# An encoder layer on one core: the order of all queues from a list scheduler inside the kernel

## The chip, the core and the metric

The kernel runs on one core of a Trainium2 chip. A core has TensorE (PE; its weight loads are shown as PEld), VectorE (DVE), ScalarE (ACT), GpSimd (POOL) and a queue on SyncE (SP) that issues nearly all transfers. Each works through its own instructions in order; semaphores tie them together. The metric is the device time of one execution in microseconds (us).

## The reference

One layer: windowed attention with a sink, and a SwiGLU feed-forward network, each between two RMS norms, with shift, scale and gate from a conditioning vector. S = 2048 tokens, D = 1024, 16 query heads and 4 key heads of 64, window of 128 tokens to both sides, hidden size 2816, all float32.

```
mod = silu(c) @ ada_w + ada_b                      # 6 x 1024: sh1, sc1, g1, sh2, sc2, g2
h   = rmsnorm(x, mix_norm_pre) * (1 + sc1) + sh1
q, k, v = split(h @ w_qkv)
logits = q k^T / 8 + bias(relative position)       # 128 queries x 384 keys, masked at +-128
p   = softmax([logits, sink])                      # the sink takes part and is dropped
x   = x + g1 * rmsnorm((p v) @ w_o, mix_norm_post)
h   = rmsnorm(x, ffn_norm_pre) * (1 + sc2) + sh2
x   = x + g2 * rmsnorm((silu(h @ w_a) * (h @ w_b)) @ w_out, ffn_norm_post)
```

## The kernel before

Activations lie transposed, features on the partitions, 512 tokens (a chunk) along the free side; there are four chunks. A float32 matmul is made from three rounded ones: each operand is split into a high part (`act.copy`) and a low part (a subtraction on VectorE or GpSimd), by `split`, lines L155 and L156, and `three`, lines L150 to L152, multiplies high by high, high by low and low by high into one PSUM bank.

The stages, in order of the program:
- The norm of chunk 0 (`nsta`, `nr`), the conditioning rows (`ada_reduce`, L263) and a first wave of q, k, v tiles (`psq`). `evac` writes q, k and v to DRAM (`q_d`, `k_d`, `v_d`), and chunks 1 to 3 follow.
- Attention: 64 units of 128 queries x 4 heads. `Unit.scores` multiplies q by k into one of two banks of the pool `psS` (`s`, L433), VectorE adds the bias and takes the maximum (L438: `pr`, `nm`), ScalarE takes the exponent (L440), GpSimd divides (L446). `Unit.values` transposes `pr` on TensorE into one of three banks (`t`, L456), splits it into `phi` and `plo` (L155, L156) and multiplies by v (`o`, L461, L462); `low` and `of` (L465, L469) put it together and write `o_d`. Between the units a budget puts in "fillers" by threes of matmuls: the q, k, v tiles of chunks 2 and 3 in the first half, the output projection (`py`, from `ol`, the loaded `o_d`, and `wo`) of chunks 0 to 2 in the second.
- The output projection of chunk 3, norms, residuals and the second normalized input `h2_d`. For chunks 2 and 3 this is done late (`late_residuals`: `ly`, `lx`, `lacc`, `nhil`, `nstl`; `ly` is multiplied by GpSimd at L508 and added to by VectorE at L509), beside the feed-forward network.
- The feed-forward network in two halves of 1024 tokens, by blocks of a 2 x 2 scheme with seven products in place of eight (`Block`, `Operands`, `Hidden`, `Outs`). Weights come in as `wiri`, sums of them as `s`, split into `wa` and `ws`; VectorE and ScalarE take the seven products out of PSUM (`take`: `p_i`, `u_i`, `b_i` for the hidden layer, `z` at L943 for the output). The hidden values go through DRAM (`g_d`).
- `finish` (L990, L991) scales each output tile and adds the residual `x1_d`.

The order of the instructions on each queue is made by the tile framework's own scheduler from the program order (the context is opened with `schedule_with_timeline_sim=True`). It is helped by hand with `tc.issue_after(...)` (an operation is held until another has been issued), `tc.high_priority(offset=...)` (it counts as that much earlier) and `tc.keep_in_program_order(...)`. Buffers are tiles of pools; a tile waits until its slot is free, pools are opened and closed in the nesting of the stages, and later pools take over the space of closed ones.

```
            for h in range(GRP):
                ps = psS.tile([P, CH], F32, tag="s", name=f"s{u}_{h}")
                ...
    psF = open_pool(ctx, "psF", 2, space=PSUM)
    psS = open_pool(att, "psS", 2, space=PSUM)
    psT = open_pool(att, "psT", 3, space=PSUM)
    psV = open_pool(att, "psV", 1, space=PSUM)
```

```
    def residual(c, k, y, xr, r, acc, alloc, eng=dve):
        sp.dma_start(xr, a["xT"][c, :, k, :])
        pool.tensor_tensor(y, y, r, ALU.mult)
        eng.tensor_tensor(y, y, xr, ALU.add)
        sp.dma_start(x1_d[c][:, k, :], y)
        ...
```

Of the kernel before, what the change touches and what calls it, by code (L numbers as in the profile page):

```python
# [11 lines left out]
F32 = mybir.dt.float32  # L12
F32R = mybir.dt.float32r
AF = mybir.ActivationFunctionType
ALU = mybir.AluOpType
# [45 lines left out]
OPERANDS = ("b11", "t2", "b21", "t3", "t1", "t4", "b22")  # L61


def f(ap):
    return ap.bitcast(F32)
# [8 lines left out]
def encoder_layer(ctx, tc, a):  # L74
# [41 lines left out]
    dve.memset(epsc, EPS)  # L116
    make_identity(nc, ident)

# [35 lines left out]
    def split(hi, lo, src, eng):  # L154
        act.copy(hi, src)  # L155
        return eng.tensor_tensor(lo, src, f(hi), ALU.subtract).ins  # L156

# [7 lines left out]
    class Chunk:  # L165
# [34 lines left out]
        def h(self, k):  # L200
            xt, c = self.xt[k], self.c
            scaled = dve.tensor_tensor(xt, xt, self.r, ALU.mult).ins
            act.activation(xt, xt, AF.Identity, bias=mod[:, k:k + 1], scale=coef[:, 0, k:k + 1])
            hi = hs.tile([P, CH], F32R, tag="hi", name=f"hi{c}_{k}")
            lo = hs.tile([P, CH], F32R, tag="lo", name=f"lo{c}_{k}")
            self.hh[k] = (hi, lo)
            return scaled, split(hi, lo, xt, dve)

    def evac(c, n, ps, psp, ptag):

        t = ev.tile([P, 2, CH], F32R, tag="e", name=f"e{c}_{n}")
        if n < KT:

            hi, lo = (t[:, i].rearrange("p (b t) -> p b t", t=P)[:, :, ::-1] for i in range(2))
            src = ps.rearrange("p (b t) -> p b t", t=P)
            act.activation(hi, src, AF.Copy, scale=DH ** -0.5)
            ins = dve.scalar_tensor_tensor(lo, src, DH ** -0.5, f(hi), ALU.mult, ALU.subtract).ins
            for j in range(2):
                h = 2 * n + j
                dst = q_d[c][h // GRP].rearrange("(i d) h t -> d i h t", i=2)[:, :, h % GRP, :]  # L220
                sp.dma_start(dst, f(t[j * DH:(j + 1) * DH]))
        elif n < KT + 2:
            ins = split(t[:, 0], t[:, 1], ps, dve)
            for j in range(2):
                for d in range(2):
                    sp.dma_start(k_d[c][2 * (n - KT) + j][d * DH:(d + 1) * DH], f(t[j * DH:(j + 1) * DH]))
        else:
            vt = nrm.tile([P, CH], F32, tag="nsq", name=f"vt{c}_{n}", bufs=2)
            act.copy(vt, ps)
            pv = psp.tile([P, CH], F32, tag=ptag, name=f"pvt{c}_{n}")  # L230
            for j in range(JB):
                pe.transpose(pv[:, j * P:(j + 1) * P], vt[:, j * P:(j + 1) * P], ident)
            t = t.rearrange("p a b -> p (a b)").rearrange("p (g j i d) -> p g j i d", g=2, j=JB, i=2)
            s = pv.rearrange("p (j g d) -> p g j d", j=JB, g=2)
            for g in range(2):
                act.copy(t[:, g, :, 0, :], s[:, g])
                ins = dve.tensor_tensor(t[:, g, :, 1, :], s[:, g], f(t[:, g, :, 0, :]), ALU.subtract).ins
                sp.dma_start(v_d[c][2 * (n - KT - 2) + g], f(t[:, g].rearrange("p j i d -> p j (i d)")))
        return ins


    with ExitStack() as pa:
# [11 lines left out]
        sp.dma_start(cb_d, cb)  # L254
        tc.keep_in_program_order(act.preload_act_table_set("natural_log_exp_and_others"))

# [25 lines left out]
        for k in range(KT):  # L282
            with tc.issue_after(steps[max(k - 2, 0)][0]) if k >= 1 else ExitStack():
                ada_reduce(*ada_load(8 + k, raws))
                ada_reduce(*ada_load(k, raws))
            dve.scalar_tensor_tensor(coef[:, 0, k:k + 1], mod[:, 8 + k:9 + k], 1.0, gains[:, 0, k:k + 1],
                                     ALU.add, ALU.mult)
            w_piece(k, 0)
            with tc.issue_after(steps[k - 2][1]) if k >= 2 else ExitStack():
                steps.append(ch0.h(k))  # L290
            for n in NORD[:WAVE]:
                three(pss[n], wres[k, n], ch0.hh[k], k == 0, k == KT - 1)
# [9 lines left out]
        def v_tile(ch, i):  # L302
# [12 lines left out]
            for m in range(2):  # L315
                t = vt[c][m][:, :, 2 * i:2 * i + 2]
                for g in range(2):
                    act.copy(t[:, g, :, 0, :], s[:, m, g])
                    ins = dve.tensor_tensor(t[:, g, :, 1, :], s[:, m, g], f(t[:, g, :, 0, :]), ALU.subtract).ins
                    if i:  # L320
                        sp.dma_start(v_d[c][2 * m + g], f(vt[c][m][:, g].rearrange("p j i d -> p j (i d)")))
# [18 lines left out]
        for i, n in enumerate(NORD[WAVE:] + NORD[:WAVE]):  # L340
            ins = qkv_tile(ch1, n)
            if i >= 2:
                with tc.issue_after(ins):
                    for w in waiting[i - 2:i - 1]:
                        ada_reduce(*w)
            if i < ADA_A:
# [64 lines left out]
    class Unit:  # L411
# [10 lines left out]
        def scores(self):  # L422
# [7 lines left out]
            for h in range(GRP):  # L430
                ps = psS.tile([P, CH], F32, tag="s", name=f"s{u}_{h}")
                for i in range(2):
                    m = pe.matmul(ps[:, :n], q[:, h, jb * P:(jb + 1) * P], kk[:, i, (jb + j0) * P:(jb + j1) * P],  # L433
                                  start=i == 0, stop=i == 1)
                    if h == i == 0:
                        self.first = m.ins
                hh = g * GRP + h
# [4 lines left out]
                if h == 0:  # L442
                    self.red = red.ins
            dve.reciprocal(rs, rs)  # L444
# [87 lines left out]
    class OProj:  # L532
# [5 lines left out]
        def fill(self, prev=None, hold=None):  # L538
# [11 lines left out]
            for n in range(KT):  # L550
# [10 lines left out]
                for k in range(KT):  # L561
                    t = o[k // 2]
                    with ExitStack() as st:
                        while hold is not None and n >= KT - HOLD and hold() is None:
                            yield None
                        if hold is not None and n >= KT - HOLD and k == 0:
                            st.enter_context(tc.issue_after(hold()))
                        three(ps, (w[:, 0, k], w[:, 1, k]), (t[:, 0, k % 2], t[:, 1, k % 2]), k == 0, k == KT - 1)
# [84 lines left out]
    for i, un in enumerate(units):  # L653
# [17 lines left out]
        if i in ADA_UNITS:  # L671
            for w in waiting:
                with tc.issue_after(un.red):
                    ada_reduce(*w)
            waiting = [ada_load(late.pop(0), ws)] if late else []
# [187 lines left out]
    def late_ada():  # L863

        for i in range(2):
# [3 lines left out]
            for t in range(5 * KT, 6 * KT):  # L869
# [10 lines left out]
                    h2_d[int(n[2]) - 1][:, 2 * k + (n[1] == "2"), :])  # L880
    with tc.high_priority(offset=1):
        half.load("b11", "t2")
# [69 lines left out]
    ops = part_ops(0, 0)  # L952
    with tc.high_priority(offset=100):
        ops.load(*OPERANDS[:2])
    with tc.high_priority(offset=400):
        block = Outs(ops, 0, 0, 0)
    for i in range(5, 7):
# [52 lines left out]

    tc.keep_in_program_order(act.preload_act_table_set("natural_log_exp_and_others"))
    NP = len(PARTS[0])
    with tc.high_priority(offset=400):
        ops.load(*OPERANDS[2:])
    end = iter(())
# [118 lines left out]
```

## Time and profile before

| | |
|---|---|
| median of 3 runs | 2156.73 us (2156.06 to 2157.14) |
| the profiled execution | 2157.47 us, span of its instructions 2155.7 us |
| TensorE busy | 95% of the span |
| VectorE, ScalarE, GpSimd busy | 76%, 50%, 34% |
| mean granted TensorE clock | 0.981 |
| moved by DMA | 396 MB, 184 GB/s |

The profile is one execution. A group of instructions is shown by its line, engine, operation and tiles (out<-in), with count, busy time, the mean duration of one in ns, the idle time of the engine ahead of them and what ended it. L150 is line 150 of the kernel. Where a table has stages, a row gives the stage in us from the start of the span, its length, the busy time of PE, PEld, DVE, ACT and POOL with the number of instructions, the granted clock, the DMA engines' busy share and GB/s.

### The profile page before, as it was taken

The numbers are of one execution on the slowest core, as the hardware profiler recorded it, in microseconds if no ns is written. First come the engines' busy times: TensorE is split into PE (matmuls) and PEld (weight loads), VectorE is DVE, ScalarE is ACT, GpSimd is POOL, SyncE is SP. The second block draws the span as 40 slices with busy tenths as digits, with TensorE's granted clock in tenths as the row PEclk, the third lists the DMA queues.
The fourth block names the chain that finished last, engine by engine and source line by source line (L and its number), as shares of the span: only waits on it lengthen the run. The fifth ranks groups of instructions, "written<-read, shape, count | busy, mean of one in ns | idle before, by whom it ended". The sixth has DMA issues, their size and how long they took to land. (4 is left out here: it accounts for less than half of the span.)

```text
span 2155.7 us, 29001 instructions
## 1 busy us (share of the span) xinstructions
PE 2037.4 (95%) x9366; PEld 1669.6 (77%) x9366; DVE 1648.5 (76%) x2933; ACT 1076.0 (50%) x2125; POOL 735.7 (34%) x687
## 2 busy tenths in 40 slices
PE   6898999999989989989999989999999999998997
PEld 4786877878777768868887867888888788877886
DVE  7656667665676669887878798777664888999987
ACT  4646666577777746343434352333332744465422
POOL 3404343367778712444354412222221000220040
PEclk9998999999999989999999999999999999999998
DMA  8887665576667695534454764323230644438442
GB/s 280 262 268 242 186 187 173 168 274 243 220 197 247 193 346 205 175 129 158 169 171 162 252 235 147 117 103 118 103 108 36 233 149 150 135 134 283 161 132 103
DMA packets 200516, 396.35 MB, mean 184 GB/s; under 512 B 20091, under 2 KB 62124, under 8 KB 195244
## 3 DMA queue, kind: packets, MB, share of 16 engines
q1 hardware_dynamic: 199788, 393.97, 54.5%
q8 instruction: 74, 1.21, 0.2%
q14 instruction: 78, 0.64, 0.1%
q10 hardware_dynamic: 576, 0.52, 0.1%
HBM read 270.65 MB, written 123.76 MB: 183 GB/s over the span
## 5 line engine op out<-in xcount | busy, mean ns | idle before, releaser
L438 DVE CUSTOM_DVE_ANT_0 pr<-s,bias,nsink 128x384 f32<-128x384 f32 (+1 forms) x256 | 149.3, 596 | 89.7 <-PE s L433 71.0
L150 PE MATMUL pc_i<-ht,ws_i 128*128 128x512 f32 x528 | 206.2, 391 | 4.9 <-DVE b_i L800 2.3
L151 PE MATMUL pc_i<-ht,ws_i 128*128 128x512 f32 x528 | 205.5, 389 | 0.0
L152 PE MATMUL pc_i<-ht,ws_i 128*128 128x512 f32 x528 | 205.3, 389 | 0.0
L440 ACT ACTIVATE pr<-pr,nm 128x385 f32<-128x385 f32 (+1 forms) x256 | 153.8, 603 | 70.7 <-DVE nm L438 65.3
L816 POOL TENSOR_TENSOR p_i<-p_i,u_i 128x512 f32<-128x512 f32 x44 | 73.5, 1671 | 307.8 <-DVE u_i L803 121.5
L446 POOL TENSOR_SCALAR pr<-pr,rs 128x384 f32<-128x384 f32 (+1 forms) x256 | 146.9, 595 | 85.3 <-DVE rs L444 85.2
L947 POOL TENSOR_TENSOR z<-z,z 128x512 f32<-128x512 f32 x32 | 53.2, 1677 | 353.0 <-DVE z L943 335.7
L433 PE MATMUL s<-k,q 128*128 128x384 f32 (+1 forms) x512 | 137.0, 361 | 21.0 <-DVE nm L438 13.7
L150 PE MATMUL pc_i<-hb,wa_i 128*128 128x512 f32 x352 | 138.1, 392 | 3.8 <-DVE u_i L790 2.6
L152 PE MATMUL pc_i<-hb,wa_i 128*128 128x512 f32 x352 | 137.5, 391 | 0.0
L151 PE MATMUL pc_i<-hb,wa_i 128*128 128x512 f32 x352 | 137.5, 391 | 0.0
L156 DVE TENSOR_TENSOR plo<-t,phi 128x512 fp32r<-128x512 f32 x184 | 121.7, 685 | 17.1 <-ACT phi L155 15.5
L155 ACT CAST ws_i<-s_i 128x512 fp32r<-128x512 f32 x132 | 81.6, 619 | 100.5 <-PE pc_i L152 91.7
L155 ACT CAST wa_i<-wiri 128x512 fp32r<-128x512 f32 x132 | 81.7, 620 | 93.8 <-PE pc_i L152 88.8
L433 PEld LDWEIGHTS s<-k,q 128*128 128x128 f32 x512 | 87.5, 195 | 45.5 <-DVE nm L438 28.1
L150 PEld LDWEIGHTS pc_i<-ht,ws_i 128*128 128x128 f32 x528 | 99.1, 188 | 28.4 <-DVE b_i L800 2.3
L456 PE MATMUL t<-ident,pr 128*128 128x128 f32 x736 | 113.7, 275 | 3.4 <-POOL pr L446 2.7
L150 PE MATMUL py<-ol,wo 128*128 128x512 f32 x256 | 103.4, 408 | 12.8 <-ACT ol L155 8.3
L152 PEld LDWEIGHTS pc_i<-ht,ws_i 128*128 128x128 f32 x528 | 99.1, 188 | 20.7
L151 PEld LDWEIGHTS pc_i<-ht,ws_i 128*128 128x128 f32 x528 | 99.1, 188 | 20.3
L156 DVE TENSOR_TENSOR wa_i<-wiri,wa_i 128x512 fp32r<-128x512 f32 x132 | 109.1, 826 | 5.1 <-ACT wa_i L155 4.9
(320 smaller groups left out, 6129.8 us busy)
## 6 DMA issues: line engine op xcount, KB each, us to landing
wiri<-w_in SPq DMA_DIRECT2D x88, 512.0 KB, 5.0
ada<-ada_w SPq DMA_DIRECT2D x40, 512.0 KB, 5.0
wiro<-w_out SPq DMA_DIRECT2D x48, 384.0 KB, 3.8
q_d<-e SPq DMA_DIRECT2D x64, 256.0 KB, 4.0
q<-q_d SPq DMA_DIRECT2D x16, 1024.0 KB, 5.4
wo<-wo_d SPq DMA_DIRECT2D x16, 1024.0 KB, 5.9
g_d_b<-p_i SPq DMA_DIRECT2D x44, 256.0 KB, 4.8
g_d_t<-p_i SPq DMA_DIRECT2D x40, 256.0 KB, 2.0
```

What stands on the lines that cost most here:

```text
L150: pe.matmul(ps, w[0], h[0], start=first, stop=False)
L151: pe.matmul(ps, w[0], h[1], start=False, stop=False)
L152: pe.matmul(ps, w[1], h[0], start=False, stop=last)
L155: act.copy(hi, src)
L156: return eng.tensor_tensor(lo, src, f(hi), ALU.subtract).ins
L433: m = pe.matmul(ps[:, :n], q[:, h, jb * P:(jb + 1) * P], kk[:, i, (jb + j0) * P:(jb + j1) * P], start=i == 0, stop=i == 1)
L438: red = dve.tensor_tensor_reduce(pr[:, h, :n], ps[:, :n], bias[g][:, h, j0 * P:j1 * P], -1.0, nsink[:, hh:hh + 1], ALU.add, ALU.min, nm[:, ...
L440: act.activation(pr[:, h, :n + 1], pr[:, h, :n + 1], AF.Exp, bias=nm[:, h:h + 1], scale=-1.0, accum_out=rs[:, h:h + 1])
L446: pool.tensor_scalar(pr[:, h, :n], pr[:, h, :n], rs[:, h:h + 1], 1.0, ALU.mult, ALU.mult)
L456: pe.transpose(pt[:, h * P:(h + 1) * P], pr[:, h, jj * P:(jj + 1) * P], ident)
L816: pool.tensor_tensor(sa, sa, b, ALU.mult)
L947: (pool if (i, x) in ((2, 2), (4, 4), (5, 5), (6, 6)) else dve).tensor_tensor(sums[hf, n2, x], sums[hf, n2, x], sums[hf, n2, y], ALU.add)
```

## The change

The computation is written as before, but against a recorder. `Recorder` stands in for the framework: every call on an engine becomes an `Op` with the regions that it reads and writes, its predecessors, and a cost from fixed constants. `place` gives every pool's tag an address by the nesting of the pools, so that closed pools' space is used again. `schedule` orders all operations on five queues in up to six rounds: `forward` is a list scheduler that always starts the operation that can start first, the more urgent one where several are ready; it gives tiles their slots, lets a VectorE operation with two SBUF inputs and a GpSimd operation not run at once (`port`), counts ScalarE's table loads, eight DMAs under way and a DMA rate; `backward` then gives each operation the latest start that the schedule allows, which is its priority in the next round. The round with the shortest planned time is kept. `emit` issues the operations in that order, with the framework's own ordering switched off (`manual_schedule`); the framework still places the semaphores. The hand-written `issue_after`, `high_priority` and `keep_in_program_order` are gone.

```
+    def cost(self, op, outs, ins):
+        ...
+        if eng == "sp":
+            op.bytes = int(np.prod(outs[0].shape)) * 4
+            op.occ, op.lat = 430, 0
+        elif eng == "pe":
+            ...
+                op.occ = n * 0.4167 + 13.5
+                op.lat = op.occ + 200
+        elif eng == "act":
+            op.occ = n / 1.2 + (51 if psum else 93)
+            op.lat = op.occ + 105
+            ...
+        elif eng == "dve":
+            fast = fn in ("tensor_copy", "tensor_scalar") and not psum
+            op.occ = n / (1.92 if fast else 0.96) + 66
+            op.lat = op.occ + 88
+            ...
+            op.port = n > P and (fast or len(sbuf) > 1)
+        else:
+            op.port = fn != "custom"
+            if fn == "tensor_tensor":
+                op.occ = n * 2.21 + 95
+                op.lat = op.occ + 45
+    ...
+    def forward(self):
+            ...
+                o = item[2]
+                if o.port:
+                    begin = max(begin, port["pool" if e == "dve" else "dve"])
+                if best is None or begin < best[0]:
+                    best = begin, e, o, src, item
+            ...
+            if e == "sp":
+                lanes.sort()
+                begin = max(begin, lanes[0])
+                first = max(begin + 1200, dma)
+                dma = first + max(o.bytes / 345.0, 100.0)
+                end = dma + 900
+                lanes[0] = end
+                lanes.sort()
+            else:
+                end = begin + o.lat
+                if o.port:
+                    port[e] = begin + o.occ
+            clock[e] = begin + o.occ
+    ...
+    def schedule(self, rounds):
+        self.place()
+        for o in self.ops:
+            o.prio = float(o.i)
+        best = None
+        for i in range(rounds):
+            order, total = self.forward()
+            if best is None or total < best[1]:
+                best = order, total, {b: b.slot for b in self.bufs.values()}
+            ...
+            if i + 1 < rounds:
+                late = self.backward(order, total)
+                for o in order:
+                    o.prio = late[o]
+        self.slots = best[2]
+        return best[0]
+    def emit(self, nc, tc, order, outside):
+        ...
+        with tc.manual_schedule():
+            for o in order:
+                if o.table == "log" and table != "log":
+                    nc.scalar.preload_act_table_set("natural_log_exp_and_others")
+                table = o.table or table
+                args, kw = [turn(x) for x in o.args], {k: turn(x) for k, x in o.kw.items()}
+                ...
+                    getattr(engs[o.eng], o.fn)(*args, **kw)
 
         for k in range(KT):
-            with tc.issue_after(steps[max(k - 2, 0)][0]) if k >= 1 else ExitStack():
-                ada_reduce(*ada_load(8 + k, raws))
-                ada_reduce(*ada_load(k, raws))
+            ada_reduce(*ada_load(8 + k, raws))
+            ada_reduce(*ada_load(k, raws))
...
-    with tc.high_priority(offset=100):
-        half.load(*[n for n in OPERANDS if n not in ("b11", "t2")])
+    half.load(*[n for n in OPERANDS if n not in ("b11", "t2")])
...
-    with tile.TileContext(nc, schedule_with_timeline_sim=True) as tc:
-        encoder_layer(tc, aps)
+    rec = Recorder(bacc())
+    ...
+    order = rec.schedule(ROUNDS)
+    ...
+    with tile.TileContext(nc) as tc:
+        rec.emit(nc, tc, order, given)
```

More of the change, by code (lines that the diff above doesn't have):

```diff
@@ L61, with __init__ @@
 OPERANDS = ("b11", "t2", "b21", "t3", "t1", "t4", "b22")
+ROUNDS = 6
+SBUF_LEFT = 1152
+SBUF_RIGHT = 229344
+BANKS = 8
+BANK = 2048
+ENGINES = ("pe", "act", "dve", "pool", "sp")
+class Op:
+    __slots__ = ("i", "eng", "fn", "args", "kw", "reads", "writes", "occ", "lat", "port", "table", "tiles", "pred", "succ",
+                 "start", "end", "prio", "npred", "ready", "ins", "bytes")
+class Buf:
+    def __init__(self, rec, name, shape, dtype, pool, tag):
+        self.name, self.shape, self.dtype, self.pool, self.tag = name, list(shape), dtype, pool, tag
+        self.row = int(np.prod(shape[1:]))
+        self.unit = 1 if self.row <= P else DH
+        self.log, self.ops, self.slot, self.real = [], set(), None, None
@@ L880, in encoder_layer @@
                     h2_d[int(n[2]) - 1][:, 2 * k + (n[1] == "2"), :])
-    with tc.high_priority(offset=1):
-        half.load("b11", "t2")
+    half.load("b11", "t2")
     lasto.close()
@@ L952, in encoder_layer @@
     ops = part_ops(0, 0)
[L953 to L956, printed above, removed]
+    ops.load(*OPERANDS[:2])
+    block = Outs(ops, 0, 0, 0)
     for i in range(5, 7):
```

437 lines of the change are left out of this document (413 added, 24 removed).

## The prediction

> **What bounds the kernel now.** I read the page first (who is busy), then the table by stage (where TensorE is idle and at what clock), then the waits of TensorE, then the timeline around the long ones.
>
> ```profile
> span 2155.7 us, 29001 instructions
> PE 2037.4 (95%) x9366; PEld 1669.6 (77%) x9366; DVE 1648.5 (76%) x2933; ACT 1076.0 (50%) x2125; POOL 735.7 (34%) x687
> ```
>
> TensorE is busy for all but 2155.7 - 2037.4 = 118.3 us, so only its idle time, and what hides behind the word busy, can be won. The stages, chosen around the idle spots (columns: length, busy time of PE, PEld, DVE, ACT, POOL, clock, DMA share, GB/s):
>
> ```profile
> core 0: us, PE busy (x) PEld busy (x) DVE busy (x) ACT busy (x) POOL busy (x), PEclk, DMA share, GB/s
> 0.00:23.00 23.00, 5.86 (x6) 1.66 (x6) 11.64 (x18) 12.01 (x17) 2.90 (x7) 1.00 0.86 311
> 172.00:182.00 10.00, 3.06 (x14) 2.35 (x12) 2.41 (x5) 0.60 (x1) 0.64 (x2) 0.80 0.97 322
> 182.00:740.00 558.00, 532.96 (x2721) 437.22 (x2720) 379.36 (x984) 396.26 (x920) 328.99 (x422) 0.99 0.63 207
> 740.00:776.00 36.00, 23.49 (x81) 17.68 (x80) 18.34 (x18) 16.50 (x22) 14.90 (x11) 0.80 1.01 354
> 925.00:948.00 23.00, 15.18 (x61) 11.81 (x61) 18.35 (x24) 7.13 (x13) 10.17 (x8) 0.88 0.33 116
> 1236.00:1346.00 110.00, 101.48 (x435) 80.36 (x434) 101.62 (x162) 43.64 (x80) 23.69 (x16) 1.00 0.57 199
> 1346.00:1686.00 340.00, 340.00 (x1502) 281.53 (x1501) 231.23 (x343) 106.30 (x184) 78.77 (x52) 1.00 0.30 103
> 1890.00:1976.00 86.00, 76.19 (x307) 58.84 (x307) 85.65 (x142) 53.20 (x106) 14.17 (x8) 0.93 0.58 202
> 2110.00:2156.00 46.00, 29.55 (x219) 27.81 (x217) 37.13 (x85) 11.62 (x27) 0.00 (x0) 0.87 0.34 121
> ```
>
> Length minus PE busy gives the idle time: head 17.1, start of attention 6.9, attention 25.0, end of attention 12.5, the late residuals 7.8, the switch to the second half 8.5, the end of the first output half 9.8, tail 16.5; together 104 of the 118, the rest in stages not shown. From 1346 to 1686 nothing is idle: 340 us that no order can shorten. Where the idle time comes in one piece the clock is low as well (0.80, 0.88, 0.93), in attention it is not (0.99). Who TensorE, and its weight loader, waited for (total, times, longest):
>
> ```profile
> PE s L433 <- DVE nm L438: 13.7, 23, 2.2
> PE py L150 <- ACT ol L155: 8.3, 2, 8.0
> PE pc_o L150 <- DVE z L943: 7.6, 2, 6.7
> PE s L433 <- DMA k<-k_d: 6.9, 1, 6.9
> PE nstl L132 <- DVE nhil L130: 6.8, 2, 5.0
> PE py L150 <- DMA wo<-wo_d: 4.4, 2, 3.5
> PEld s L433 <- DVE nm L438: 28.1, 49, 2.6
> ```
>
> So there are two kinds of loss: one long stall at each change of stage, and 49 short ones in attention, where a score matmul waits until VectorE has read one of two score banks. What a long stall costs beyond itself:
>
> ```profile
> 763.51 0.39 PE L151 MATMUL py<-ol,wo 128*128 128x512 f32 x1
> 763.74 0.39 PE L152 MATMUL py<-ol,wo 128*128 128x512 f32 x1
> 772.16 1.22 PE L150 MATMUL py<-ol,wo 128*128 128x512 f32 x2 [8.04 <-ACT ol L155]
> 774.02 0.63 PE L152 MATMUL py<-ol,wo 128*128 128x512 f32 x1
> 774.44 0.63 PE L150 MATMUL py<-ol,wo 128*128 128x512 f32 x1
> 777.43 0.63 PE L152 MATMUL py<-ol,wo 128*128 128x512 f32 x1
> ```
>
> Start to start is 0.23 us before the stall and 0.42 after it, for nine rows and the merged ones beside them: some 11 matmuls x 0.2 = 2.2 us more. The first two rows also show that "busy" hides idle time: a matmul shows 0.39 us and the next starts after 0.23, so a gap under 0.16 us is no idle time on the page. That is why the loader shows 28.1 us of waiting for the score banks where the array shows 13.7.
>
> **The change, part by part.** The built programs hold the same arithmetic: 9350 matmuls, the same VectorE, ScalarE and GpSimd operations but for three ScalarE table loads fewer, 1226 DMAs on the SP queue. What moves is the order on each queue and which buffer a tile gets. Waiting instructions: GpSimd 310 to 350, VectorE 1020 to 1035, ScalarE 805 to 785, TensorE 281 to 276. I cost these at nothing, because TensorE, the busiest, has not more; if each of the 15 on VectorE and 40 on GpSimd cost even 0.1 us, it would be 5.5 us, on engines that are 76% and 34% busy. From the first hidden block on TensorE's own order stays almost the same; there only the others' orders can help.
>
> *Attention (182 to 740).* In the built order I added up the matmuls (0.23 us each for 512 columns, less in proportion for narrower ones) that stand between the end of a score and the score that takes its bank again. Before, 32 of 254 such distances are under 0.9 us; after, 1. Under 1.2 us: 53 against 22. The chain that must fit in is the read of the bank, and two hand-overs:
>
> ```profile
> L438 DVE CUSTOM_DVE_ANT_0 pr<-s,bias,nsink 128x384 f32<-128x384 f32 x224 | 134.4, 613 | 73.5 <-PE s L433 59.6 <-PE t L456 10.3 <-POOL pr L446 2.3
> L155 ACT CAST phi<-t 128x512 fp32r<-128x512 f32 x184 | 100.8, 589 | 22.1 <-PE t L456 17.3 <-PE o L461 3.4
> L156 DVE TENSOR_TENSOR plo<-t,phi 128x512 fp32r<-128x512 f32 x184 | 121.7, 685 | 17.1 <-ACT phi L155 15.5
> ```
>
> 613 ns and the hand-overs are about 1 us, so most of the 28.1 us goes: I take 24 (16 if the short distances were not all that stalled, 28 at most). Of the other 25.0 - 13.7 = 11.3 us of idle time I take 8. Against that stands a price: the value matmuls now follow their transposes closely. The median distance from the fourth transpose of a bank to the first value matmul falls from 6.0 to 2.0 us, to the second from 6.7 to 2.8, where phi and plo need 0.589 + 0.685 = 1.27 us and hand-overs. I take 5 us back for the closest of the 184. Net: 27 (0 to 40).
>
> *Start of attention.* The two loads of the first keys are late because the SP queue is in order:
>
> ```profile
> 162.50 9.20 SPq L221 DMA_DIRECT2D q_d<-e  x6
> 171.76 0.59 SPq L398 DMA_DIRECT2D q<-q_d  x1
> 174.58 1.12 SPq L407 DMA_DIRECT2D k<-k_d  x1
> ```
>
> Stores of q, each waiting for its evacuation, stand ahead of the loads. After, the loads of q, of the own keys, of v and of the bias stand 30 to 50 places earlier, and the load of the neighbour's keys (L407) three places behind their stores and ahead of ten stores of q, where eight stood ahead of it. The 6.9 us go, and the clock's 2.2: 9 (4 if DMA, at 322 GB/s here, is itself the limit).
>
> *End of attention.* Before, the four loads of the last block's attention output stand together behind the weights; after, three of four stand ahead of the last store, and the first block's weight preparation has moved into attention. The waits for ol and wo are 8.3 + 4.4 = 12.7 us, the clock's share after two stalls 4.4. But the DMA engines are full here (share 1.01, 354 GB/s), and moved loads only help as far as they spread into the 0.63 before. I take 10 (0 to 17).
>
> *Late residuals.* VectorE is at the head of a chain of queues:
>
> ```profile
> 928.24 0.32 SPq L510 DMA_DIRECT2D x_d<-ly  x1
> 928.61 0.42 SPq L841 DMA_DIRECT2D ly<-y_d  x1
> 933.99 1.73 DVE L509 TENSOR_TENSOR ly<-ly,lx 128x512 f32<-128x512 f32 x1 [3.19 <-POOL ly L508]
> ```
>
> The second ly is loaded only behind the store of the first, which waits for VectorE; then VectorE waits 3.19 us with the evacuations of PSUM queued behind it. After, both loads stand ahead of that store, and the statistics matmul stands 10 places later. Of 7.8 idle and 2.2 by clock I take 9 (3 to 10).
>
> *End of the first output half.* VectorE is full (85.65 of 86 us), and its order is poor:
>
> ```profile
> 1962.19 4.91 DVE L990 TENSOR_TENSOR z<-z,nrz 128x512 f32<-128x512 f32 x8
> 1973.88 0.70 DVE L943 TENSOR_TENSOR z<-pc_o,z 128x512 f32<-128x512 f32 x1
> ```
>
> Eight scalings that nobody needs soon stand ahead of an evacuation that TensorE awaits for 6.7 us. After, the first such evacuation stands in front of the last of them and some twelve weight splits fewer stand in the stretch. VectorE is still full there: 7 of the 9.8 and the clock's share (0 to 12).
>
> *The lock.* The planner keeps a VectorE operation with two SBUF inputs off GpSimd's:
>
> ```profile
> 18.44 2.20 POOL L156 TENSOR_TENSOR w<-wqkv,w 128x896 fp32r<-128x896 f32 x1 [17.14 <-ACT w L155]
> 18.75 2.44 DVE L142 TENSOR_TENSOR nr<-nr,nta 128x512 f32<-128x512 f32 x1
> ```
>
> The DVE operation, as wide as plo's 0.685, lasts until just after GpSimd's. Here it is worth 1.7 us on the head's chain; later it is inside the items above. *Head, stages not shown, half switch, tail*: 2, 3, 2 and 2. The half switch has VectorE busy 101.6 of 110 us with splits that wait for buffers, the head is loads (311 GB/s), and the tail is VectorE work in a chain. They are bound by the amount of work or of bytes, which stays, so I give each of the four -3 to 5.
>
> Sum: 27 + 9 + 10 + 9 + 7 + 9 = 71 us. The profiled execution took 2157.5, its span 2155.7, the median is 2156.7; 2157.5 - 71 = **2086 us**. With every high end (40, 9, 17, 10, 12 and four times 5) it is 108 us, 2049; where attention gives nothing and the rest holds, 2113.
>
> [...]
>
> **The rivals.**
> *The transitions stay.* For it: DMA is at 0.97 and 1.01 of its time at both ends of attention, VectorE at 85.65 of 86 in the output; order does not make either faster. Against: the stalls before have a queue's order as their cause in the rows above. Attention gains 27, the rest 7: 2123.
> *Attention becomes too tight.* The value matmuls' chain has 2.8 - 1.27 = 1.5 us at the median for hand-overs and for what ScalarE and VectorE do first; two foreign operations of 0.6 us use that up, and TensorE then stands at each bank with one filler matmul to bridge it. At 0.6 us for each of 184 banks in place of my 5 us in all: 2086 + 110 - 5 = 2191, slower than before. It decides from (71 + 5) / 184 = 0.41 us per bank on. For it: every distance is planned from constants, and one late operation delays all behind it. Against: ScalarE and VectorE are busy 71% and 68% of attention, and those distances were planned with both queues counted.
> *The clock falls in attention.* If many short stalls lowered it from 0.99 to the 0.88 of the row at 925, the 533 busy us would take 533 x (1/0.88 - 1) = 73 more and eat the gain: 2159, no change. Against: 49 short waits leave it at 0.99 now. [...]
> That the change does nothing is no rival: the built orders differ on every queue.
>
> **How the numbers follow.** Forecast 0.64 (its own range 2049 to 2113), transitions stay 0.17, too tight 0.14, clock 0.05. About 0.2% can be told from no change. Faster: 0.64 + 0.17 = 0.81; same 0.05; slower 0.14. The range takes in the first two, 0.81: from 2048 (every high end) to 2140 (the transition rival with attention at 10 in place of 27).
>
> **What would show it.** Right: PE idle time of some 60 us, the waits of s for nm under 5 us on the loader, no wait of s for k, of nstl or of z over 3 us, clock 0.9 or better around 740 to 776. Wrong: waits of o for plo or phi in the tens of us (too tight), clock under 0.95 within attention, or the same 7 to 8 us stalls at its two ends.

## The result, and the profile after

The changed kernel takes 2092.42 us (median of 4 runs, 2089.79 to 2096.39), the kernel before 2156.39 in the same comparison: 64.0 us less, ratio 0.9706, 95% interval 0.9689 to 0.9724. The forecast was 2086 us, the range 2048 to 2140. The profiled execution took 2096.4 us, the slowest of the four, and its span is 61.1 us shorter than before. All figures by stage, here and below, are read from one execution of each kernel; the executions of one kernel differ by 7 us (the changed one, above) to 10 us (the kernel before, 2150.38 to 2160.76 beside experiment 1), so two or three us in one stage are not told from that. First the page of the changed kernel, the lines that answer to the first fence of the prediction. `emit` issues every operation through one line, so all its instructions carry L586, and a PSUM tile is called "bank".

```profile
span 2094.6 us, 29028 instructions
PE 2012.7 (96%) x9366; PEld 1664.9 (79%) x9366; DVE 1649.6 (79%) x2933; ACT 1069.9 (51%) x2122; POOL 755.9 (36%) x687
```

TensorE's idle time fell from 118.3 to 81.9 us, its busy time by 24.7: fewer gaps too short to count as idle (the loader waits 10.3 us for `nm` where the array shows 6.6, before 28.1 and 13.7), and fewer matmuls at a low clock (mean granted clock 0.990, before 0.981). VectorE does the same work in the same time. For the table by stage I cut both traces at the same matmuls (both have 9366 in nearly the same order), so that a stage holds equal work. The changed kernel, then four stages of the kernel before, in the columns of the prediction's table:

```profile
core 0: us, PE busy (x) PEld busy (x) DVE busy (x) ACT busy (x) POOL busy (x), PEclk, DMA share, GB/s
161.50:206.60 45.10, 42.72 (x201) 34.57 (x201) 32.03 (x63) 30.15 (x61) 15.80 (x18) 1.00 0.72 222
206.60:718.50 511.90, 497.39 (x2602) 417.95 (x2601) 357.71 (x935) 374.45 (x875) 322.60 (x409) 0.99 0.67 219
718.50:818.70 100.20, 93.00 (x402) 73.79 (x402) 83.21 (x110) 65.72 (x107) 35.59 (x22) 0.98 0.83 303
864.00:909.40 45.40, 45.40 (x202) 37.58 (x201) 42.21 (x53) 18.20 (x30) 22.85 (x15) 1.00 0.47 161
1181.40:1318.20 136.80, 136.56 (x601) 112.42 (x600) 119.41 (x185) 53.28 (x99) 36.50 (x22) 1.00 0.54 188
1819.00:1926.90 107.90, 97.42 (x401) 77.33 (x400) 98.08 (x167) 65.33 (x127) 28.18 (x9) 0.95 0.61 198
```

```profile
154.90:206.40 51.50, 43.65 (x201) 35.86 (x200) 34.25 (x78) 28.72 (x67) 19.79 (x25) 0.90 0.76 254
738.50:850.30 111.80, 98.24 (x401) 78.48 (x400) 80.50 (x102) 66.88 (x104) 34.80 (x22) 0.92 0.82 289
1226.40:1374.30 147.90, 139.38 (x602) 111.73 (x601) 128.71 (x200) 55.89 (x103) 37.78 (x25) 1.00 0.56 196
1876.40:1985.80 109.40, 99.59 (x402) 77.93 (x402) 109.05 (x182) 66.56 (x131) 18.74 (x10) 0.92 0.59 206
```

What each stage gained, by the starts of its first and last matmul in the two traces, beside the prediction's term (us, lengths between edges rounded to 0.1 as in the rows above, gains from unrounded times; minus is a loss):

| stage | matmuls | before | after | gain | predicted |
|---|---|---|---|---|---|
| head, to the first `psq` | 0 to 6 | 23.5 | 27.8 | -4.3 | 2 |
| up to attention | 6 to 600 | 131.4 | 133.7 | -2.3 | in "stages not shown" |
| start of attention | 600 to 800 | 51.5 | 45.1 | 6.4 | 9 |
| attention | 800 to 3400 | 532.1 | 511.9 | 20.1 | 27 |
| end of attention | 3400 to 3800 | 111.8 | 100.2 | 11.7 | 10 |
| late residuals | 4000 to 4200 | 56.7 | 45.4 | 11.3 | 9 |
| half switch | 5400 to 6000 | 147.9 | 136.8 | 11.0 | 2 |
| end of the first output half | 8200 to 8600 | 109.4 | 107.9 | 1.4 | 7 |
| tail | 8600 on | 169.9 | 167.7 | 2.2 | 2 |
| all others | | | | 3.5 | 3, with the stage up to attention |
| sum | | 2155.7 | 2094.6 | 61.1 | 71 |

The largest waits of TensorE and of its weight loader in the changed kernel (total, times, longest):

```profile
PE bank L586 <- ACT hi L586: 14.4, 2, 13.1
PE bank L586 <- DVE nsq L586: 8.6, 3, 5.7
PE bank L586 <- DVE nm L586: 6.6, 6, 2.3
PE bank L586 <- DVE zacc L586: 5.6, 2, 4.2
PE bank L586 <- ACT z L586: 5.1, 3, 4.4
PE bank L586 <- DVE nhia L586: 4.4, 1, 4.4
PEld bank L586 <- ACT phi L586: 10.5, 25, 1.8
PEld bank L586 <- DVE nm L586: 10.3, 14, 2.6
```

The waits of 6.9 us for `k` and 5.0 for `nhil` are gone, the longest for `ol` is 2.8 where it was 8.0, and those for `nm` went from 28.1 to 10.3 on the loader. The 13.1 for `hi` (8.0 before) and the 8.6 for `nsq` (9.1 and 0.5 before) are the head. The 4.4 for `nhia` lies in the stage up to attention, where the kernel before has no such wait. The 4.2 and 4.4 for `zacc` and `z` lie at the end of the first output half.

**The head.** VectorE's queue in the changed kernel around `nr`, for which the first `psq` waits (start, duration):

```profile
17.11 3.10 DVE L586 CUSTOM_DVE_ANT_0 ada<-ada,cb,adab 128x1024 f32<-128x1024 f32 x1 [0.89 <-DMA ada<-ada_w]
21.20 1.28 DVE L586 CUSTOM_DVE_ANT_0 ada<-ada,cb,adab 128x1024 f32<-128x1024 f32 x1
22.41 2.55 DVE L586 TENSOR_TENSOR nr<-nr,nta 128x512 f32<-128x512 f32 x1
```

Four conditioning rows stand ahead of `nr`, the last two of them shown; in the kernel before it is two. The first one shown lasts 3.10 us beside a GpSimd split of 2.07 (the row ahead of it, with no GpSimd operation beside it, took 1.28), and `nr` lasts 2.55 beside the next split, of 2.44, where it took 0.68 in run 1: what the planner counts as the lock shows twice here. Over the fourteen traces of this case the first `psq` starts at 22.4 to 23.7 us where two rows stand ahead of `nr` (eight traces), at 25.3 with three (one), and at 27.0 to 29.6 with four (five).

**The end of the first output half.** The sums `z<-z,z` of GpSimd over this kernel (count, then shortest, median and longest in ns), and from VectorE's timeline the first and the last of 29 operations in a row and what followed (... marks those left out):

```profile
L586 POOL TENSOR_TENSOR z<-z,z x32: 1282/1612/15127, 1792.5 to 2042.9; 128x512 f32<-128x512 f32 x32
```

```profile
1854.82 0.55 DVE L586 TENSOR_TENSOR ws_o<-s_o,ws_o 128x384 fp32r<-128x384 f32 x1
...
1868.47 0.56 DVE L586 TENSOR_TENSOR ws_o<-s_o,ws_o 128x384 fp32r<-128x384 f32 x1
1872.12 6.21 DVE L586 TENSOR_TENSOR zacc<-zacc,zsq 128x512 f32<-128x512 f32 x4 [3.09 <-ACT zsq L586]
```

One addition that takes 1282 ns at its shortest took 15,127. It began at 1855.05 and ended 1.14 us after VectorE's last operation in that row had ended: it lasted through 29 operations with two SBUF inputs, none of which was slowed (0.55 or 0.56 us for each of 384 columns, from the first to the last). The same shows in runs 1, 4, 6, 7 and 10 below: one such addition takes 11.2 to 15.7 us beside 21 to 30 operations in a row, and each time it ends 1.15 us after the last of them. `forward` never lets the two run at once, so in the plan VectorE pauses for it; but a planned pause becomes no wait: `emit` hands down an order, the framework's semaphores follow the data, and VectorE ran on. VectorE's operation of 1854.82 had begun 0.23 us before the addition, and the addition's 15.1 us reach over the whole row.

The wait of 4.4 us for `z` in this stage has another cause. The evacuation stood on ScalarE behind a cast that waited for its load:

```profile
1896.71 0.62 ACT L586 CAST hb21o<-hb21o 128x512 fp32r<-128x512 f32 x1 [2.66 <-DMA hb21o<-g_d_b]
1897.24 1.55 ACT L586 COPY z<-bank 128x512 f32<-128x512 f32 x3
```

### The profile page after: what moved, and what is told of

It is laid out like the page before. It is cut to its first block, busy times and chain, and to the rows that moved or that the text cites. A ratio compares the mean times of both kernels' runs of the same rounds, so it can differ in the third digit from the quotient of the medians.

```text
span 2094.6 us, 29028 instructions
## 1 busy us (share of the span) xinstructions
PE 2012.7 (96%) x9366; PEld 1664.9 (79%) x9366; DVE 1649.6 (79%) x2933; ACT 1069.9 (51%) x2122; POOL 755.9 (36%) x687
## 5 line engine op out<-in xcount | busy, mean ns | idle before, releaser
L586 PE MATMUL bank<-ht,ws_i 128*128 128x512 f32 x1584 | 373.5, 389 | 0.0
L586 PEld LDWEIGHTS bank<-ht,ws_i 128*128 128x128 f32 x1584 | 297.2, 188 | 62.1 <-DVE p_i L586 0.5
L586 PE MATMUL bank<-hb,wa_i 128*128 128x512 f32 x1056 | 253.6, 389 | 0.7 <-DVE u_i L586 0.7
L586 PEld LDWEIGHTS bank<-hb,wa_i 128*128 128x128 f32 x1056 | 198.0, 188 | 42.7 <-DVE u_i L586 1.6
L586 PE MATMUL bank<-ol,wo 128*128 128x512 f32 x768 | 210.7, 403 | 6.1 <-ACT ol L586 4.3
L586 POOL TENSOR_SCALAR pr<-pr,rs 128x384 f32<-128x384 f32 (+1 forms) x256 | 156.8, 629 | 140.7 <-DVE rs L586 140.7
L586 ACT ACTIVATE pr<-pr,nm 128x385 f32<-128x385 f32 (+1 forms) x256 | 155.3, 608 | 82.7 <-DVE nm L586 78.0
L586 POOL TENSOR_TENSOR z<-z,z 128x512 f32<-128x512 f32 x32 | 65.3, 2061 | 345.4 <-DVE z L586 182.2
L586 DVE CUSTOM_DVE_ANT_0 pr<-bank,bias,nsink 128x384 f32<-128x384 f32 (+1 forms) x256 | 147.6, 595 | 51.4 <-PE bank L586 49.7
L586 POOL TENSOR_TENSOR p_i<-p_i,u_i 128x512 f32<-128x512 f32 x44 | 73.7, 1676 | 274.6 <-DVE u_i L586 142.3
L586 PEld LDWEIGHTS bank<-ol,wo 128*128 128x128 f32 x768 | 144.2, 191 | 34.9 <-ACT ol L586 5.1
L586 DVE TENSOR_TENSOR u_i<-bank,u_i 128x512 f32<-128x512 f32 x176 | 120.5, 684 | 45.5 <-PE bank L586 45.5
L586 DVE TENSOR_TENSOR plo<-bank,phi 128x512 fp32r<-128x512 f32 x184 | 119.2, 685 | 36.6 <-ACT phi L586 35.1
L586 PE MATMUL bank<-k,q 128*128 128x384 f32 (+1 forms) x512 | 133.2, 346 | 6.7 <-DVE nm L586 6.6
L586 ACT CAST ws_i<-s_i 128x512 fp32r<-128x512 f32 x132 | 81.8, 620 | 107.8 <-PE bank L586 93.3
L586 PE MATMUL bank<-hi,ws 128*128 128x512 f32 x384 | 135.8, 402 | 0.1
L586 DVE TENSOR_TENSOR wa_i<-wiri,wa_i 128x512 fp32r<-128x512 f32 x132 | 111.4, 845 | 29.4 <-ACT wa_i L586 29.2
L586 ACT CAST wa_i<-wiri 128x512 fp32r<-128x512 f32 x132 | 81.8, 620 | 91.4 <-PE bank L586 91.4
L586 PE MATMUL bank<-ht,wa_i 128*128 128x512 f32 x528 | 126.8, 389 | 0.0
L586 PE MATMUL bank<-hb,ws_i 128*128 128x512 f32 x528 | 126.8, 389 | 0.0
L586 DVE TENSOR_TENSOR ws_i<-s_i,ws_i 128x512 fp32r<-128x512 f32 x132 | 115.0, 871 | 3.9 <-ACT ws_i L586 3.9
L586 PE MATMUL bank<-hi,w 128*128 128x512 f32 x320 | 103.4, 402 | 14.4 <-ACT hi L586 14.4
```

Source lines behind the costliest of these rows:

```text
L586: getattr(engs[o.eng], o.fn)(*args, **kw)
```

## The experiments

What I wanted to know: what in the planner brings the gain (priorities, lock, transfer model, hand-overs), whether the causes that the prediction read from the trace of before are the causes, and where 71 became 61.

**1. One round, so no slack priorities.**

```
-ROUNDS = 6
+ROUNDS = 1
```

> The changed kernel with one round of forward in place of six: among operations that are ready the one written first in the program is taken, not the one with the least slack; lock, costs and slots as before. Theory (the slack of backward places the loads and the splits ahead of the changes of stage, and most of the 64 us rests on it): the half switch and the two ends of attention get their stalls back, 2092 + 20 to 35 us, so 2112 to 2127. Rival (any order that starts what can start first does it, the priorities matter little): 2092 within 8 us. The head: theory for its loss (the conditioning row c is loaded ninth because of its slack) says the first psq matmul starts earlier here than 27.8 us, by 2 to 4; the rival (the squares and two table loads bind) says it stays at 27.8.

Measured: 2133.02 us, 41 more than the changed kernel. By stages the changed kernel's gain is lost at the start of attention (8.6 us), in attention (15.7) and at the late residuals (6.9). In the output matmuls 8000 to 8200 lose 5.9 and those from 8600 on 8.1, while the end of the first output half between them is 5.0 shorter. The gain stays at the end of attention (0.2 us faster) and at the half switch (0.8 faster). So of 64 us the slack order brings 41, and the rest comes without it; the theory had the loss at the half switch and both ends of attention, and only the start of attention lost. At the head the conditioning vector `c` is loaded first here, and the first `psq` starts at 29.6 us: the load's place isn't the cause.

**2. The lock taken out of the plan.**

```
-            op.port = n > P and (fast or len(sbuf) > 1)
-            op.port = fn != "custom"
+    op.port = False                            # for every operation
```

> The changed kernel whose planner knows nothing of the VectorE/GpSimd lock (port is False for every operation); all else stays. Theory 1 (the planned turns come true on the chip, and knowing them is worth something): VectorE and GpSimd operations meet, more of them last as long as the one of the other engine, and the whole takes 2092 + 5 to 25 us. Theory 2 (the turns are a plan only, no wait enforces them; the six z additions at 3.8 us each in the first output half show that VectorE runs ahead all the same): no more than 4 us either way.

Measured: 2104.65 us, 12 more, as theory 1 has it. But its mechanism is not there. The page of this kernel:

```profile
PE 2018.2 (96%) x9366; PEld 1666.8 (79%) x9366; DVE 1644.4 (78%) x2933; ACT 1069.5 (51%) x2122; POOL 730.3 (35%) x687
```

VectorE and GpSimd are busy for 5.2 and 25.6 us less than with the lock in the plan: they lose no more time to each other without it. (The first line above also shows that the plan counted VectorE's copies and scalings within SBUF, `fast`, and not only its operations with two SBUF inputs.) By stages it loses 12.4 us at the start of attention, 7.6 at the late residuals and 5.7 at the half switch, and gains 8.3 in the stage up to attention, 3.7 in attention and 5.7 at its end. The last experiment takes the lock out a second time.

**3. The `z` sums on VectorE.**

```
-(pool if (i, x) in ((2, 2), (4, 4), (5, 5), (6, 6)) else dve).tensor_tensor(
+dve.tensor_tensor(
...
```

> The changed kernel with the sixteen z<-z,z additions of the output stage moved from GpSimd to VectorE (0.68 us each there; six of them took 22.73 us on GpSimd at the end of the first output half, and TensorE waited 4.2 us for zacc and 4.4 for z behind them). Theory (GpSimd starves beside a VectorE that issues two-input operations back to back, and this ate what the end of the first output half should have gained): the matmuls 8200 to 8600 come 5 to 8 us earlier against after, 2092 - 6 = 2086. Rival (VectorE is full in that stretch, with 85.65 of 86 us before, and 8 x 0.68 = 5.4 us more are simply added): 2092 to 2098.

(There are 32 such sums, sixteen in each half of the tokens, and the edit moves all of them. The six took 22.73 us because of the one at 15.1; the other five took 1.28 to 1.75.) Measured: 2083.71 us. Matmuls 8200 to 8600 take 4.1 us less, fewer than the 5 to 8 of the theory, and the waits for `zacc` and `z` are gone, but another took their place there:

```profile
PE bank L586 <- ACT wa_o L586: 8.2, 1, 8.2
PE bank L586 <- DVE wa_o L586: 3.1, 2, 1.7
```

The two traces lie 11.2 us apart, and most of that comes from stages that the edit doesn't touch, 4.3 us from attention alone: the plan is a new one from end to end. Nor is the starved addition shown to be what this stage lost. Runs 4, 6, 7 and 10 leave the sums on GpSimd, one of them takes 13.1 to 15.7 us there, and the same matmuls gain 5.7, 3.8, 4.2 and 4.3 us all the same; in run 2 the longest sum takes 3.6 us and they take 109.4. Run 8 is run 7 with the sums on VectorE, and there they take 0.8 us more.

**4. A slower DMA in the plan.**

```
-dma = first + max(o.bytes / 345.0, 100.0)
+dma = first + max(o.bytes / 300.0, 100.0)      # and in backward
```

> The changed kernel whose planner counts 300 bytes per ns of DMA in place of 345; what is computed and loaded stays. Theory (in the stages before attention the transfers run at 266 to 300 GB/s, so the plan expects loads earlier than they come and every operation behind a late one waits; a plan with the measured rate puts them in a better order): the stages up to the start of attention (matmul 600) gain 3 to 8 us against after, the rest within 3 us, so 2085 to 2092. Rival (those stages are bound by the bytes, whatever the plan says): 2092 within 3 us; a plan that expects too little of the DMA may also begin loads too early elsewhere and lose 2 to 5 us.

Measured: 2081.12 us. The stages up to matmul 600 gain 8.4 us, attention 6.7 that I had not expected, and matmuls 3800 to 4000 lose 11.5. The head starts its first `psq` at 22.8 us. Its loads go out in the order of the changed kernel (`c` ninth), but on VectorE `nr` now stands ahead of the third conditioning row:

```profile
17.61 0.43 DVE L586 TENSOR_SCALAR nta<-nta 128x512 f32<-128x512 f32 x1
18.08 2.44 DVE L586 TENSOR_TENSOR nr<-nr,nta 128x512 f32<-128x512 f32 x1
```

So the loads' order is not the cause of the head's loss; it goes with the rows ahead of `nr` on VectorE, four in run 1 and two here.

**5. In the kernel before, both loads of a pair ahead of the first store.**

```
-for k in range(KT):
-    sp.dma_start(y, y_d[c - CPH][:, k, :])
-    residual(c, k, y, temp(f"lx{c}_{k}"), r, acc, temp)
+for k in range(0, KT, 2):
+    # loads of ly and lx for k and k + 1, then both residuals
```

> The kernel before, with one thing moved: in the late residuals both y and both x of a pair are loaded ahead of the store of the first sum, so the second load is no longer queued on SP behind a store that waits for VectorE. Theory of the prediction (this queue order is what makes the late residuals lose 11 us): the stalls at 925 to 948 (5.0 for nhil, 3.0 for p_i, and the clock's share) go, 2157 - 8 to 11 = 2146 to 2149. Rival (the loads come late for another reason, or VectorE is late anyway): within 3 us of 2157.

Measured: 2151.61 us, ratio 0.9976 (0.9964 to 0.9988), between the two. By the medians the whole gained 6.0 us; the two traces lie 3.3 apart. At the late residuals themselves it gained 2.6 us of the 11. The wait for `p_i` went, the one for `nhil` stayed. The waits there, and VectorE's queue ahead of `nhil`:

```profile
PE nstl L132 <- DVE nhil L130: 4.3, 1, 4.3
PE pc_i L150 <- DVE u_i L791: 1.2, 1, 1.2
```

```profile
938.69 0.68 DVE L799 TENSOR_TENSOR u_i<-pc_i,u_i 128x512 f32<-128x512 f32 x1
939.29 0.68 DVE L801 TENSOR_TENSOR b_i<-pc_i,u_i 128x512 f32<-128x512 f32 x1
939.89 0.42 DVE L130 CAST nhil<-lacc 128x512 fp32r<-128x512 f32 x1
```

The sum `lacc` was complete at 930.9; `nhil` stood behind 9 us of splits and evacuations, and TensorE, which had put the statistics matmul next, waited. So by these traces the store ahead of the load costs some 2.6 us, which the spread of the executions could hide. The wait that is left comes from where `nhil` stands on VectorE and `nstl` on TensorE; moving those was not tried.

**6. A longer hand-over in the plan.**

```
-return q.lat + (60 if q.eng != op.eng else 0)
+return q.lat + (150 if q.eng != op.eng else 0)  # and the 60s in forward and backward
```

> The changed kernel whose planner counts 150 ns for a hand-over between engines in place of 60. Theory (in attention the plan is a little too tight: its short waits of the weight loader for nm, phi and plo come to 29 us and the matmuls 800 to 3400 lose 14 us against the gain forecast): attention gains 3 to 8 us, the whole 2085 to 2089. Rival (the plan is not tight, the waits are covered by the next weight load): within 4 us of 2092, and where the order changes elsewhere up to 10 us either way.

Measured: 2080.38 us; attention gained 7.5 us. But run 4, with 60 ns, gained 6.7 there. That the hand-over is the reason is not shown; a different plan is enough.

**7, 8. A later landing; and three edits together.**

```
-end = dma + 900
+end = dma + 1600                               # and 2100 to 2800 in backward
```

> The run with 300 bytes per ns, and besides 0.7 us more from the issue of a transfer to its landing in the plan (its late residuals stalled 10.5 us at 842.9 because ly landed 3.8 us after its issue, where the plan had 2.9). Theory: the stall at the late residuals goes and the rest stays, 2081 - 8 to 11 = 2070 to 2073. Rival (the late residuals are a chain of queues that any small shift upsets; where this one goes another comes): 2078 to 2084.

> The changed kernel with the three edits together: the sixteen z additions on VectorE, 300 bytes per ns, 0.7 us more to the landing. If the gains add up: 2092 - 11 (300 bytes per ns) - 4 (z at the end of the first output half, matmuls 8200 to 8600) - 9 (late residuals) = 2068. If each new plan only deals out its losses anew: 2075 to 2085.

Measured: 2083.51 and 2083.07 us. The stall stayed (9.1 us for `p_i`), so the landing is not its cause, and single gains do not add up: five different plans, runs 3, 4, 6, 7 and 8, lie between 2080 and 2084.

**9. In the kernel before, three banks for scores and two for transposes.**

```
-psS = open_pool(att, "psS", 2, space=PSUM)
+psS = open_pool(att, "psS", 3, space=PSUM)
-psT = open_pool(att, "psT", 3, space=PSUM)
+psT = open_pool(att, "psT", 2, space=PSUM)
```

> The kernel before with three PSUM banks for the scores and two for the transposes, where it has two and three; its own scheduler orders the queues. Theory of the prediction (the 28.1 us that the weight loader waits for nm in attention come from a score that takes a bank again too soon): those waits fall under 10 us and attention, from the 800th to the 3400th matmul, takes 532 - 8 to 20 us, if two transpose banks do. Rival (VectorE is simply late in attention, the banks only show it): the waits for nm go over into waits of the transposes for plo and pr, attention stays within 5 us of 532 or gets longer.

Measured: 2166.28 us, ratio 1.005 (1.0033 to 1.0067). The loader's waits between 182 and 740:

```profile
PEld o L462 <- DVE plo L156: 12.7, 26, 1.6
PEld o L461 <- ACT phi L155: 11.6, 19, 3.1
PEld t L456 <- DVE plo L156: 8.5, 11, 1.9
PEld s L433 <- DVE nm L438: 8.0, 27, 1.1
```

The 28.1 us for `nm` fell to 8.0, and matmuls 800 to 3400 took 5.8 us more: the waits went over to `plo` and `phi`, 24.3 us in the two rows of `o`, where they were 10.6, and 8.5 at the transposes, where there were none to speak of. One bank fewer for the transposes is part of that, so the run doesn't say what three score banks alone would bring, nor how much time the 28.1 us of waiting are worth.

**10. The late residuals one hidden block later.**

```
-            next(late, None)
+            for _ in range(1 if hf else (0 if t == 0 else 2 if t == 8 else 1)):
+                next(late, None)
```

> The run with 300 bytes per ns, and besides the late residuals begin one hidden block later (none beside the first block, two steps beside the ninth). Theory (its stall of 10.5 us at 842.9 comes from the ring of ten temporary tiles, handed out in program order: the first hidden blocks' tiles wait for the tiles of the residuals, which wait for their loads; the loss is already in the plan, the landing has no part in it): the matmuls 3800 to 4000 take 45.4 us where that run took 56.8, and the whole 2081 - 8 to 12 = 2069 to 2073. Rival (VectorE and the SP queue are full there, the stall only moves by a block): 2079 to 2084.

Measured: 2075.00 us, ratio 0.9628 (0.9614 to 0.9642). Matmuls 3800 to 4000 take 45.3 us, as expected, and the wait of 10.4 us of run 4 is gone; TensorE's only wait left between 781 and 900 is this:

```profile
PE bank L586 <- ACT p_i L586: 2.1, 1, 2.1
```

The whole gained 6 us, not 8 to 12: of the 11.5 us some came back late in attention (2.4, matmuls 2800 to 3400), at its end (1.3), in matmuls 4000 to 5000 (2.0) and at the end of the first output half (1.4).

**11. All these edits together** (of runs 3, 6, 7 and 10; the two DMA constants count as one where four edits are spoken of).

> The changed kernel with the z additions on VectorE, 300 bytes per ns, 0.7 us more to the landing, a hand-over of 150 ns, and the late residuals one block later. If the plan's constants decide: faster than each of the runs with one of them, 2065 to 2075. If a new plan only deals out the losses at the changes of stage anew: 2076 to 2084.

Measured: 2069.16 us, ratio 0.9602 (0.9588 to 0.9616), faster than each run with some of them. The end of the first output half, 107.9 us in the changed kernel, is down to 93.4, with VectorE full from end to end and no GpSimd in it:

```profile
1806.70:1900.10 93.40, 92.48 (x401) 74.55 (x401) 93.40 (x169) 61.75 (x120) 0.00 (x0) 1.00 0.67 234
```

**12. The same without the lock in the plan.**

> The run with the four edits, with a planner that knows nothing of the VectorE/GpSimd lock. In the pair before (the changed kernel with and without the lock) the run without it was 12 us longer, though VectorE and GpSimd were busy no longer (1644.4 and 730.3 against 1649.6 and 755.9 us). Theory 1 (the time that the lock takes up has to be in the plan, whether or not the turns come true: without it the plan expects every evacuation too early): again 8 to 20 us longer than the four edits, 2077 to 2089. Theory 2 (the 12 us were one of the chance shifts of 5 to 10 us that any new plan brings): 2069 within 6 us.

Measured: 2059.72 us, ratio 0.9540 (0.9524 to 0.9556): 9 us shorter than with the lock, against both theories. It is the fastest kernel of this study, 32.7 us below the changed one.

```profile
span 2061.0 us, 28986 instructions
PE 2001.4 (97%) x9366; PEld 1662.7 (81%) x9366; DVE 1645.2 (80%) x2965; ACT 1073.3 (52%) x2122; POOL 682.7 (33%) x655
```

Run 11 has VectorE busy for 1660.9 us, this one for 1645.2. Taking the lock out cost 12 us in one pair and won 9 in the other, and VectorE was busy for less in both. So nothing here shows that knowing the lock is worth anything in this planner, whose turns are not enforced. The start of attention, which lost 12.4 us in the first pair, gains 3.4 in this one, and the end of attention gains 5.9. Why these two pairs differ in sign stays open; some of it may be what any new plan brings, which moved single stages by some 10 us either way.

## Why the prediction was right, and where its steps were off

The forecast held: faster, 61 us of span against 71, and in the places given, the changes of stage and attention. Order is the reason as far as the waits show it; no run separates it from the other thing that changed, which buffer a tile gets. The rivals fell. *Transitions stay*: start and end of attention gained 18.1 us although DMA is still busy 0.72 and 0.83 of the time there (0.76 and 0.82 before, by the same matmuls). *Too tight*: the loader's waits for `phi` rose only from 3.8 to 9.1 us and those for `plo` stayed (6.8, now 6.9), about the 5 us that I took back. *The clock falls*: 0.99 in attention, and at its end, for the 400 matmuls above, 0.98 where it was 0.92. By its own list of what would show it: no wait of `s` for `k` and no 8 us stalls is right; idle time of 81.9 in place of 60, 10.3 us for `nm` in place of under 5, and 4.4 for `z` are not.

The steps that failed:

- *Attention, 27, measured 20.1.* I turned 24 of the 28.1 us of the loader's waits for `nm` into time. Only 17.8 of them went; with that in place of 24 the sum would have been 20.8. That a wait of the loader is worth its length in time was an assumption and stays one: run 9 took 20.1 us of these waits away and put others in their place, and attention got longer.
- *Half switch, 2, measured 11.0.* The step was that VectorE is busy for 101.6 of 110 us and that the amount of work stays. By the same matmuls it had 128.71 us of work in 147.9; now it has 119.41 in 136.8: 9.3 us less. Little of that was done earlier, most was put off: adding up its operations, VectorE has done 2.1 us more than before when matmul 5400 starts, 8.7 less at matmul 6000 and 2.4 less at 6600. Five conditioning rows are among what moved behind matmul 6000. What TensorE waited for in the kernel before, between 1226 and 1376, were evacuations that stood behind splits on their queues:

```profile
PE pc_i L150 <- DVE b_i L800: 3.3, 3, 1.7
PE pc_i L150 <- DVE u_i L790: 3.2, 4, 1.3
PE pc_i L150 <- ACT p_i L787: 1.1, 1, 1.1
```

  In the changed kernel TensorE idles there for 0.24 us. Run 1 keeps this gain without slack priorities. VectorE's work filled 87% of this stage, before and after, and did not bind it, as some of it could be done at another time; in run 1 these 600 matmuls took 136.0 us, 0.227 each, the pace of the prediction's rows ahead of a stall (0.23).
- *Head, +2, measured -4.3.* "Bound by the amount of work" was wrong here too, with the other sign: four conditioning rows ahead of `nr` where there had been two.
- *End of the first output half, 7, measured 1.4.* The work did leave VectorE, from 109.05 us to 98.08. The step that failed is that TensorE's wait there would go with it: the 6.7 us for `z` went, and 4.2 for `zacc`, behind the starved GpSimd addition, and 4.4 for `z`, behind a load, came. How much the addition costs stays open: taking the sums off GpSimd gave 4.1 us in run 3 and -0.8 between runs 7 and 8, and the 14.6 of run 11 come with three other edits.
- *The lock, counted inside other items.* It gave nothing that can be shown.
- *Late residuals, 9, measured 11.3.* The size was about right; of the cause I gave, run 5 bears out some 2.6 us.
- *Start of attention, 9, measured 6.4, and end of attention, 10, measured 11.7.* The waits for `k` and `wo` went as forecast, and the longest for `ol` shrank. What moved them, the queue's order or buffers that come free sooner, wasn't tried alone.

The misses at the head and the half switch nearly cancel (-6.3 and +9.0), which is luck; attention and the output half make up the shortfall (-7 and -5.6). With all terms the forecast is 6.4 us below the median.

## What to carry to other kernels

A list scheduler over recorded operations finds order at the changes of stage that hand-placed priorities had not, and most of what it found here (41 of 64 us) comes with the slack priorities. Here the plan reached the chip as an order and not as times: nothing enforced a planned pause, VectorE ran 29 operations in a row through one, and the GpSimd addition that the plan had kept apart from them took 15.13 us, where the shortest takes 1.28. Try several constants and keep the fastest on the chip: single edits moved one stage by 5 to 12 us, gains from separate runs did not add up, and a plan's own reasons for a gain are worth checking before they are believed.

## What was unexpected about the hardware

A GpSimd addition of 128x512 that takes 1.28 us at its shortest took 15.13 us beside 29 VectorE operations in a row, none of which was slowed; in five other runs one took 11.2 to 15.7 us beside 21 to 30 of them. The other way round VectorE's `nr`, 0.68 us in run 1, took 2.55 in the changed kernel and 2.44 in run 4, beside a GpSimd split of 2.44 and 2.20 that had begun before it.
